# A hybrid decoder layer: the seven-product form of matrix multiplication in part of the first SwiGLU and nearly all of the second

## The chip, the cores and the metric

The kernel runs on one core of a Trainium2 chip. The metric is the device time of one execution in microseconds (us). A core has five engines that run beside each other, each in the written order of its own instructions: TensorE (PE: matrix products), VectorE (DVE), ScalarE (ACT), GpSimd (POOL) and SyncE (SP, which here issues the large transfers). They meet only by semaphores.

## The reference

The layer takes x (512 positions by 1024 features, float32) and computes, with RMSNorm as x times 1/sqrt(mean x^2 + eps) times a gain g:

```
h = x + 1/2 * SwiGLU_1(RMSNorm(x))        SwiGLU(y) = (silu(y @ w1) * (y @ w3)) @ w2
u = RMSNorm(h); y_s5, y_gla, gates from u @ W_in
h = h + W_out( sigmoid(gate_s5) * (y_s5 @ P_s5) + sigmoid(gate_gla) * (y_gla @ P_gla) )
h = h + 1/2 * SwiGLU_2(RMSNorm(h))
out = RMSNorm_final(h)
```

The hidden width is 2816, which is 22 features of 128 ("feature f" below is such a block of 128 columns of w1 and w3 with the matching 128 rows of w2). S5 is a diagonal state-space branch whose constants (discretised eigenvalues and their powers) are computed inside the kernel from its parameters; GLA is a chunked linear attention.

## The kernel before

Positions lie along the free axis, features on partitions: h is eight tiles of 128 x 512. Every product is made in split precision: an operand is written as a rounded high part and a low part (value minus high part), and `mm3` (L227) adds three matmuls: high x high, high x low, low x high. ScalarE makes the high copies and VectorE subtracts for the low ones; a subtraction that makes a weight's low part is called a low here.

The whole layer is a list of units (L63). A unit is one weight tile: it is loaded (`load`, L240, on SyncE's queue, five units ahead), split into high and low (`split`, L250, three units ahead), multiplied (`mm`), and followed by its `post`. The main loop at the end of `_body` walks the list, and this walk writes the order of each engine: at unit n it emits the load of n + 5, the matmuls of n, the split of n + 3, tasks and fetches that are due (`run_tasks`, L280), the post, and then one step of each generator that is attached to n by `side` (L978). Rings give five raw tiles, four high and four low ones, four PSUM banks `mm` and four banks `sp`.

The first SwiGLU (`ffn`, L303) takes the features in groups of 6, 6, 5 and 5 (GROUPS1). Each feature is two units, w1 and w3, of 24 matmuls of 512 columns each; behind the second stands `g_post` (L307), a chain of VectorE and ScalarE steps that applies the norm's factor b, silu and the product and splits the result into a pair. After a group its part of w2 follows: eight units, one for each tile of h. The first two of these wait for the group's last feature only with their last matmuls. The norm's factor b is asked for behind the fourth unit (`at_lead`, L424).

The S5 constants (`s5_prep`, L449) are 56 steps of small VectorE work, GpSimd copies (L608) and ScalarE copies. A step writes complex powers into one of two pairs of tiles (`cmul`, L578), and GpSimd copies out of them. The steps are spread over the units of the first SwiGLU from its seventh unit on, about one a unit.

In the second SwiGLU (`ffn_seven`, L1426) features 0 to 5 are classic and 6 to 21 use a seven-product form (Strassen and Winograd) of the 2 x 2 block product [w1; w3] by the halves of the normalized h: a feature is then seven products of 12 matmuls of 256 columns, 84 in all where the classic one has 48 of 512 columns. Its weight sums are made by VectorE tasks and its right-hand operands, called X, by `seven_x` (L1351) once, in the units behind the start of this SwiGLU; they are built from h times gain times b. The w2 parts of the group before stand between the products. The posts combine the seven results (`post_1` to `post_7`).

## Time and profile before

| | |
|---|---|
| median of 3 runs | 1068.77 us (1067.56 to 1069.32) |
| the profiled execution | 1067.78 us |
| its span in the trace | 1066.1 us |
| TensorE busy | 1052.4 us, 99% of the span |
| VectorE busy | 717.4 us, 67% |
| ScalarE busy | 438.3 us, 41% |
| GpSimd busy | 65.2 us |
| moved by DMA | 101.41 MB, 95 GB/s on average |

The span runs from the first to the last instruction that the profiler saw; 1.7 us of the execution lie outside it. Busy times of matmuls are modelled and overlap, so rates are read from starts, not from durations. The share of busy time is an average over stages: the first SwiGLU, the mixing layer, the second SwiGLU.

### The profile page before, as it was taken

What the parts mean: (1) busy time and instruction counts of PE and PEld (TensorE: products, weight loads), DVE (VectorE), ACT (ScalarE), POOL (GpSimd) and SP (SyncE); (2) the same over time, 40 slices, a digit from 0 to 9 for tenths busy, and PEclk for the clock granted to TensorE, in tenths of its full rate; (3) what the DMA queues carried; (4) which work ended last, traced back from release to release, by engine and by line L of the source; (5) the groups of instructions that cost most, each with busy time, mean ns of one, the idle gap of its engine ahead of it and who ended that gap; (6) DMA issues with size and microseconds to landing.
All of it is one profiled execution on the core that took longest, in us unless ns stands there. A gap on an engine that the chain in (4) does not pass through costs nothing.

```text
span 1066.1 us, 14475 instructions
## 1 busy us (share of the span) xinstructions
PE 1052.4 (99%) x5548; PEld 906.4 (85%) x5548; DVE 717.4 (67%) x1403; ACT 438.3 (41%) x779; POOL 65.2 (6%) x118
## 2 busy tenths in 40 slices
PE   9999999999999999999999999999999999999996
PEld 7888888888888898888878888888899999999996
DVE  6688654797644555687385755557886778777866
ACT  7323254322222433553645233434444444454444
POOL 4002600100400000001000000000000000000000
PEclk9999999999999999999999999999999999999998
DMA  7423223322422322122122222222133233333222
GB/s 260 123 61 134 79 75 103 127 85 62 149 86 62 112 102 79 60 80 79 60 80 80 80 98 99 100 79 89 60 104 105 89 110 101 107 100 109 82 78 79
DMA packets 34388, 101.41 MB, mean 95 GB/s; under 512 B 4096, under 2 KB 5568, under 8 KB 34320
## 3 DMA queue, kind: packets, MB, share of 16 engines
q1 hardware_dynamic: 33408, 99.17, 27.9%
q0 software_dynamic: 480, 0.79, 0.3%
q8 instruction: 43, 0.70, 0.3%
q10 hardware_dynamic: 432, 0.54, 0.1%
q14 instruction: 25, 0.20, 0.1%
HBM read 98.19 MB, written 2.10 MB: 94 GB/s over the span
## 4 chain that ended last, share of the span: by engine, by line
PE 95%; ACT 2%; DVE 1%; DMA 1%; issue 0%; SPq 0%; DVEq 0%; ACTq 0%
PE mm L228 20%; PE mm L230 20%; PE mm L229 20%; PE mm L1541 5%; PE mm L1540 5%; PE mm L1538 5%; PE sp L228 4%; PE sp L229 4%; PE sp L230 4%; ACT g L105 1%; PE sp L999 1%; PE sp L1001 1%; PE sp L1000 1%; PE mm L1001 1%; PE mm L1000 1%; PE mm L999 1%
## 5 line engine op out<-in xcount | busy, mean ns | idle before, releaser
L228 PE MATMUL mm<-g,hi 128*128 128x512 f32 x944 | 374.3, 396 | 0.0
L230 PE MATMUL mm<-g,lo 128*128 128x512 f32 x944 | 369.7, 392 | 0.0
L229 PE MATMUL mm<-g,hi 128*128 128x512 f32 x944 | 369.5, 391 | 0.0
L84 DVE TENSOR_TENSOR lo<-raw,hi 128x1024 fp32r<-128x1024 f32 (+3 forms) x176 | 198.6, 1133 | 130.7 <-ACT hi L105 130.3
L105 ACT ACTIVATE g<-g 128x512 f32<-128x512 f32 (+4 forms) x227 | 130.5, 582 | 338.6 <-DVE g L84 327.2
L105 ACT ACTIVATE hi<-raw 128x1024 fp32r<-128x1024 f32 (+3 forms) x176 | 170.2, 974 | 109.9 <-PE mm L229 64.5
L230 PEld LDWEIGHTS mm<-g,lo 128*128 128x128 f32 x944 | 177.7, 188 | 40.6
L229 PEld LDWEIGHTS mm<-g,hi 128*128 128x128 f32 x944 | 177.9, 188 | 37.1
L228 PEld LDWEIGHTS mm<-g,hi 128*128 128x128 f32 x944 | 177.9, 188 | 37.1
L84 DVE TENSOR_TENSOR g<-g,g 128x512 fp32r<-128x512 f32 (+7 forms) x341 | 181.6, 551 | 38.5 <-ACT g L105 32.1
L84 DVE TENSOR_TENSOR g<-mm,g 128x512 f32<-128x512 f32 (+1 forms) x104 | 58.2, 564 | 47.3 <-PE mm L1541 17.2
L228 PE MATMUL sp<-g,g 128*128 128x512 f32 (+1 forms) x176 | 65.7, 373 | 0.0
L229 PE MATMUL sp<-g,g 128*128 128x512 f32 (+1 forms) x176 | 65.4, 372 | 0.0
L230 PE MATMUL sp<-g,g 128*128 128x512 f32 (+1 forms) x176 | 65.0, 370 | 0.0
L84 DVE TENSOR_TENSOR g<-g,mm 128x512 f32<-128x512 f32 (+1 forms) x72 | 44.3, 623 | 19.7 <-PE mm L230 15.2
L105 ACT ACTIVATE g<-mm 128x256 f32<-128x256 f32 (+1 forms) x51 | 19.7, 386 | 91.4 <-PE mm L1541 78.1
L1541 PE MATMUL mm<-b,lo 128*128 128x256 f32 x192 | 53.7, 279 | 0.0
L1541 PE MATMUL mm<-g,lo 128*128 128x256 f32 x192 | 53.6, 279 | 0.0
L1538 PE MATMUL mm<-b,hi 128*128 128x256 f32 x192 | 53.6, 279 | 0.0
L1540 PE MATMUL mm<-b,hi 128*128 128x256 f32 x192 | 53.6, 279 | 0.0
L1538 PE MATMUL mm<-g,hi 128*128 128x256 f32 x192 | 53.5, 279 | 0.0
L1540 PE MATMUL mm<-g,hi 128*128 128x256 f32 x192 | 53.5, 279 | 0.0
(177 smaller groups left out, 1260.2 us busy)
## 6 DMA issues: line engine op xcount, KB each, us to landing
raw<-win SPq DMA_DIRECT2D x24, 512.0 KB, 3.4
raw<-w1b SPq DMA_DIRECT2D x22, 512.0 KB, 3.4
raw<-w3b SPq DMA_DIRECT2D x22, 512.0 KB, 3.5
raw<-w1a SPq DMA_DIRECT2D x21, 512.0 KB, 3.4
raw<-w3a SPq DMA_DIRECT2D x21, 512.0 KB, 3.6
raw<-w2b SPq DMA_DIRECT2D x32, 256.0 KB, 2.6
raw<-w2a SPq DMA_DIRECT2D x16, 384.0 KB, 3.1
raw<-w2a SPq DMA_DIRECT2D x16, 320.0 KB, 2.8
```

The lines of the kernel that those rows point to most:

```text
L84: V.tensor_tensor(out=out, in0=x, in1=y, op=op)
L105: S.activation(out, x, f, **kw)
L228: PE.matmul(out, lhsT=wh, rhs=xh, start=start, stop=False)
L229: PE.matmul(out, lhsT=wh, rhs=xl, start=False, stop=False)
L230: PE.matmul(out, lhsT=wl, rhs=xh, start=False, stop=stop)
L999: PE.matmul(banks[i], lhsT=xh, rhs=wh, start=(k == 0), stop=False)
L1000: PE.matmul(banks[i], lhsT=xh, rhs=wl, start=False, stop=False)
L1001: PE.matmul(banks[i], lhsT=xl, rhs=wh, start=False, stop=(k == KT - 1))
L1538: PE.matmul(bank, lhsT=wh[:, c], rhs=xh[k], start=start and k == 0, stop=False, skip_group_check=True)
L1540: PE.matmul(bank, lhsT=wh[:, c], rhs=xl[k], start=False, stop=False, skip_group_check=True)
L1541: PE.matmul(bank, lhsT=wl[:, c], rhs=xh[k], start=False, stop=k == 3, skip_group_check=True)
```

## The change

In the first SwiGLU features 0 to 3 stay classic, 4 to 11 take the seven-product form, and 12 to 21 are classic again in two groups of 5. The classic ones need the split x that the seven-product operands do not leave room for, so `again` reads x a second time and splits it anew. In the second SwiGLU feature 0 is classic and 1 to 21 take the seven-product form, in groups of 2, 4, 4, 4, 4 and 4. The operands X are built from h times gain, without b: in the first SwiGLU in the units from the third to the tenth, in the second beside the last product of the mixing layer. So the norm's factor has to be multiplied in behind the products: `post_2` and `post_3` get a multiplication by b before silu, and the finished value gets one too. The factor of the first norm is asked for behind the third unit rather than the fourth. The S5 preparation starts with feature 12, two steps to a unit in 28 units; its three large tiles are allocated there, since X takes their places before. Rows of w1 and w3 are stored in another order.

```diff
-GROUPS1 = [6, 6, 5, 5]
-GROUPS2 = [6, 4, 4, 4, 4]
+GROUPS1 = [4, 4, 4]
+GROUPS1_REST = [5, 5]
+GROUPS2 = [2, 4, 4, 4, 4, 4]
+ORDER_K = [0, 2, 4, 6, 1, 3, 5, 7]
+PLACE_K = [ORDER_K.index(k) for k in range(8)]
...
-    m_t, co_re, co_im = big(), big(), big()
+    m_t = co_re = co_im = None
...
-            c = k * stride + off
+            c = place[k] * stride + off
...
-    f1 = ffn(a["w1a"], a["w3a"], a["w2a"], GROUPS1, "n1", lead1, finish_ffn1)
-    at_lead(f1, "n1", 3)
...
+    def seven_x(X, g):
...
+        for j in range(4):
+            even, odd = get(), get()
+            for x, k in ((even, 2 * j), (odd, 2 * j + 1)):
+                act(x, h[k], AF.Copy, scale=g[:, k:k + 1])
+            low()
+            yield
+            ta, tb = get(), get()
+            sub(ta[:, left], even[:, right], even[:, left])
+            sub(ta[:, right], odd[:, right], ta[:, left])
+            split(even[:, left], 1, j, -1.0)
+            split(odd[:, left], 2, j)
+            yield
+            low()
+            sub(tb[:, left], even[:, right], odd[:, right])
+            sub(tb[:, right], odd[:, left], ta[:, right])
+            split(ta[:, right], 6, j)
+            split(ta[:, left], 5, j)
+            yield
+            low()
+            split(tb[:, left], 7, j)
+            split(tb[:, right], 4, j)
+            split(odd[:, right], 3, j, -1.0)
+        yield
+        low()
+        yield
+    def ffn_seven(w1, w3, w2, X, groups, classic, norm_key, lead, end):
...
+            def post_2():
+                x = v["x"] = get()
+                sub(x[:, left], v["c"][:, left], be)
+                mul(x[:, left], x[:, left], st[norm_key].b[:, left])
+                soon(1, lambda: act(x[:, left], x[:, left], AF.Silu, scale=-1.0))
...
+            def post_4():
+                x = v["x"]
+                gs[f] = pair()
+                mul(x[:, left], al, x[:, left])
+                if final:
+                    mul(x[:, left], x[:, left], st[norm_key].b[:, left])
...
+            def post_3():
+                x = v["x"]
+                add(x[:, right], ga, v["u"][:, left])
+                mul(x[:, right], x[:, right], st[norm_key].b[:, right])
+                soon(1, lambda: act(x[:, right], x[:, right], AF.Silu, scale=-1.0))
+                c = right if final else slice(0, T)
+                soon(2, lambda: (mul(x[:, right], v["c"][:, right], x[:, right]),
+                                 mul(x[:, c], x[:, c], st[norm_key].b[:, c])))
+                split_g(c, 3)
...
+        if classic == groups[0]:
+            fill = parts(0)
+            for _ in range(4):
+                next(fill)
+        for q in range(0 if fill is None else 1, len(groups)):
...
+        if end is None:
+            tail_units(w2, sum(groups[:-1]), groups[-1], gs)
+        else:
+            end()
+            for _ in parts(len(groups) - 1, 4):
+                pass
+        return first
+    def again():
+        due = len(units)
+        def fetch(k, box):
+            box.append(raws.take())
+            for i in range(2):
+                nc.sync.dma_start(out=box[0][:, i * T:(i + 1) * T], in_=a["x"][k + i])
+        def high(k, box):
+            xs[k] = pair()
+            act(xs[k][0], box[0][:, k % 2 * T:(k % 2 + 1) * T], AF.Copy, scale=g1[:, k:k + 1])
+        def low(k, box):
+            stt(xs[k][1], box[0][:, k % 2 * T:(k % 2 + 1) * T], g1[:, k:k + 1], xs[k][0].bitcast(F32), ALU.mult,
+                ALU.subtract)
+            if k % 2:
+                raws.drop(box[0])
+        for k in range(0, KT, 2):
+            box = []
+            fetches.append((due - 6 + 2 * k, [raws], lambda k=k, box=box: fetch(k, box)))
+            for i in range(2):
+                tasks.append((due + 2 + k + i, [], lambda k=k + i, box=box: high(k, box)))
+                tasks.append((due + 3 + k + i, [], lambda k=k + i, box=box: low(k, box)))
+    X1 = {}
+    f1 = ffn_seven(a["w1a"], a["w3a"], a["w2a"], X1, GROUPS1, GROUPS1[0], "n1", lead1, again)
+    at_lead(f1, "n1", 2)
+    rest1 = len(units)
+    ffn(a["w1a"], a["w3a"], a["w2a"], sum(GROUPS1), GROUPS1_REST, "n1", finish_ffn1)
...
+        nonlocal m_t, co_re, co_im
+        m_t, co_re, co_im = big(), big(), big()
...
-    f2 = ffn_seven(a["w1b"], a["w3b"], a["w2b"], GROUPS2, "n2", lead2)
+    X2 = {}
+    f2 = ffn_seven(a["w1b"], a["w3b"], a["w2b"], X2, GROUPS2, 1, "n2", lead2, None)
...
+    x1 = seven_x(X1, g1)
+    for n, times in ((2, 1), (3, 2), (4, 2), (5, 2), (6, 2), (7, 2), (8, 1), (9, 2)):
+        side(f1 + n, *[x1] * times)
+    x2 = seven_x(X2, g2)
+    for n, times in ((1, 1), (2, 1), (3, 2), (4, 1), (5, 2), (6, 1), (7, 2), (8, 2), (9, 1), (10, 1)):
+        side(mix_out + n, *[x2] * times)
...
-    spots, n = [], f1
-    for nk in GROUPS1:
-        spots.extend(range(n + 6 if n == f1 else n, n + 2 * nk - 3))
+    spots, n = [], rest1
+    for nk in GROUPS1_REST:
+        spots.extend(range(n, n + 2 * nk - 3))
         spots.extend(range(n + 2 * nk + 1, n + 2 * nk + 8))
         n += 2 * nk + 8
-    spots = spots[:-5]
...
-            o[w + s] = c(g[f"{n}_{w}"][0].reshape(8, 128, 22, 128).transpose(2, 1, 0, 3)).reshape(22, 128, 1024)
+            o[w + s] = c(g[f"{n}_{w}"][0].reshape(8, 128, 22, 128)[ORDER_K].transpose(2, 1, 0, 3)).reshape(22, 128,
+                                                                                                           1024)
```

In the program that is built the first remaining group begins at unit 112 (feature 12) and its w2 part at unit 122; the second group's units are 130 to 147.

Below is VectorE's order at two places. The names are tiles by their program number; `lo` is a low of a weight, `g` a general tile, `mm` and `sp` are PSUM banks. The first place is the S5 preparation where GpSimd copies out of the tile pair that `cmul` writes. Before (here g_862 and g_863 are one such pair, written in turn with the other half of the same tiles):

```order
L84 TENSOR_TENSOR lo_73<-raw_65,hi_69 128x1024
L84 TENSOR_TENSOR g_102<-g_102,mm_88 128x512
L84 TENSOR_TENSOR g_864<-g_862,g_472 128x256
L84 TENSOR_TENSOR g_864<-g_863,g_472 128x256
L84 TENSOR_TENSOR g_862<-g_864 128x256
L84 TENSOR_TENSOR g_864<-g_863,g_472 128x256
L84 TENSOR_TENSOR g_864<-g_862,g_472 128x256
L84 TENSOR_TENSOR g_863<-g_864 128x256
L84 TENSOR_TENSOR lo_74<-raw_66,hi_70 128x1024
L84 TENSOR_TENSOR g_103<-g_103,mm_89 128x512
L84 TENSOR_TENSOR lo_75<-raw_67,hi_71 128x1024
```

One step of six instructions stands between two lows, beside one addition to h from the w2 part. In the changed kernel, from the low of unit 121 on:

```order
L87 TENSOR_TENSOR lo_73<-raw_64,hi_69 128x1024
L87 TENSOR_TENSOR g_2440<-g_2209,g_2223 128x256 x2
L87 TENSOR_TENSOR g_2438<-g_2440 128x256
L87 TENSOR_TENSOR g_2440<-g_2209,g_2223 128x256 x2
L87 TENSOR_TENSOR g_2439<-g_2440 128x256
L87 TENSOR_TENSOR g_2440<-g_2438,g_2223 128x256
L87 TENSOR_TENSOR g_2440<-g_2439,g_2223 128x256
L87 TENSOR_TENSOR g_2438<-g_2440 128x256
L87 TENSOR_TENSOR g_2440<-g_2439,g_2223 128x256
L87 TENSOR_TENSOR g_2440<-g_2438,g_2223 128x256
L87 TENSOR_TENSOR g_2439<-g_2440 128x256
L87 TENSOR_TENSOR lo_74<-raw_65,hi_70 128x640
```

Two steps of six stand between two lows, the first two steps that write the pair from the constants c (g_2209) and onward, and behind the second low the chain of feature 15 follows.

The second place is the start of the first SwiGLU, behind the first two feature chains. Before:

```order
L84 TENSOR_TENSOR g_380<-mm_88,g_367 128x512
L96 SCALAR_TENSOR_TENSOR g_382<-mm_89,g_367 128x512
L84 TENSOR_TENSOR g_380<-g_382,g_381 128x512
L84 TENSOR_TENSOR g_388<-g_380,g_387 128x512
L84 TENSOR_TENSOR lo_72<-raw_67,hi_68 128x1024
L84 TENSOR_TENSOR g_418<-mm_90,g_367 128x512
L96 SCALAR_TENSOR_TENSOR g_420<-mm_91,g_367 128x512
```

The chain of feature 1 (four instructions on g_380), a low, and the next chain. In the changed kernel:

```order
L87 TENSOR_TENSOR g_360<-mm_85,g_347 128x512
L87 TENSOR_TENSOR g_362<-mm_86,g_347 128x512
L87 TENSOR_TENSOR g_360<-g_362,g_361 128x512
L87 TENSOR_TENSOR g_368<-g_360,g_367 128x512
L87 TENSOR_TENSOR g_371<-g_306 128x256
L87 TENSOR_TENSOR g_371<-g_307,g_371 128x256
L99 SCALAR_TENSOR_TENSOR b_375<-g_306,b_375 128x256
L87 TENSOR_TENSOR b_377<-g_307,b_377 128x256
L87 TENSOR_TENSOR g_372<-g_306,g_307 128x256
L87 TENSOR_TENSOR g_372<-g_307,g_371 128x256
L87 TENSOR_TENSOR lo_75<-raw_66,hi_71 128x1024
L87 TENSOR_TENSOR g_341<-raw_67,g_340 128x256
```

The same chain (on g_360), then six steps of 256 columns for the operands X, a low, and the first low part of a weight for product 1's feature; the next chain comes eight further instructions on.

## Rows read from the trace of the kernel before

**Rows 1.** The page's first part: busy us, share of the span, instructions of each engine.

```profile
PE 1052.4 (99%) x5548; PEld 906.4 (85%) x5548; DVE 717.4 (67%) x1403; ACT 438.3 (41%) x779; POOL 65.2 (6%) x118
```

**Rows 2.** Timeline of TensorE: start us, length, line, operation, shapes, count.

```profile
727.80 0.39 PE L229 MATMUL mm<-g,hi 128*128 128x512 f32 x1
...
744.96 0.39 PE L229 MATMUL mm<-g,hi 128*128 128x512 f32 x1
...
856.34 0.28 PE L1538 MATMUL mm<-b,hi 128*128 128x256 f32 x1
...
859.05 0.28 PE L1541 MATMUL mm<-g,lo 128*128 128x256 f32 x1
```

**Rows 3.** Windows: stretch, its length, busy us of each engine, granted clock, DMA.

```profile
850.00:900.00 50.00, 50.00 (x354) 46.76 (x353) 38.88 (x70) 24.45 (x51) 0.00 (x0) 1.00 0.28 99
```

**Rows 4.** Timelines of TensorE and VectorE at the head; idle and releaser in brackets.

```profile
18.87 0.39 PE L228 MATMUL mm<-g,hi 128*128 128x512 f32 x1
...
24.85 3.49 DVE L84 TENSOR_TENSOR lo<-raw,hi 128x1024 fp32r<-128x1024 f32 x3
...
37.54 0.69 DVE L84 TENSOR_TENSOR g<-sp,g 128x512 f32<-128x512 f32 x1 [3.20 <-ACT g L105]
...
40.94 0.68 DVE L84 TENSOR_TENSOR g<-mm,g 128x512 f32<-128x512 f32 x1
```

**Rows 5.** Timeline of VectorE: first rows of the preparation's steps 3 to 8, and ends.

```profile
60.53 0.26 DVE L84 TENSOR_TENSOR g<-s5p,g 128x16 f32<-128x16 f32 x2
...
67.15 0.58 DVE L100 TENSOR_SCALAR g<-g 128x16 f32<-128x16 f32 x3
...
69.76 0.96 DVE L84 TENSOR_TENSOR lo<-raw,hi 128x768 fp32r<-128x768 f32 x1
...
85.70 0.17 DVE L102 TENSOR_SCALAR g<-g 128x16 f32<-128x16 f32 x1
...
87.75 0.95 DVE L84 TENSOR_TENSOR lo<-raw,hi 128x768 fp32r<-128x768 f32 x1
...
89.22 0.17 DVE L100 TENSOR_SCALAR g<-g 128x16 f32<-128x16 f32 x1
...
92.07 0.95 DVE L84 TENSOR_TENSOR lo<-raw,hi 128x768 fp32r<-128x768 f32 x1
...
93.54 0.25 DVE L84 TENSOR_TENSOR g<-g 128x16 f32<-128x16 f32 x2
...
95.61 0.95 DVE L84 TENSOR_TENSOR lo<-raw,hi 128x768 fp32r<-128x768 f32 x1
...
97.07 0.75 DVE L84 TENSOR_TENSOR g<-g,g 128x256 f32<-128x256 f32 x2
```

**Rows 6.** Timelines of GpSimd and VectorE: the copies, and a write that waits for them.

```profile
98.35 27.24 POOL L608 COPY g<-g 64x64 f32<-64x64 f32 x64 [54.75 <-DVE g L84]
...
119.47 0.43 DVE L84 TENSOR_TENSOR g<-g 128x256 f32<-128x256 f32 x1 [1.51 <-POOL g L608]
```

**Rows 7.** Windows during the copies: PE, PEld, DVE, ACT, POOL busy with instructions.

```profile
98.35:103.85 5.50, 5.50 (x26) 4.52 (x25) 5.33 (x11) 1.06 (x1) 5.03 (x12) 1.00 0.43 156
...
114.85:120.35 5.50, 5.50 (x26) 4.51 (x25) 3.10 (x7) 0.83 (x2) 4.85 (x15) 1.00 0.51 186
```

**Rows 8.** Timeline of VectorE: a step of 256 columns with a squaring, and what follows.

```profile
218.38 2.47 DVE L84 TENSOR_TENSOR g<-g,g 128x256 f32<-128x256 f32 x6
...
222.24 1.22 DVE L84 TENSOR_TENSOR lo<-raw,hi 128x1024 fp32r<-128x1024 f32 x1
```

**Rows 9.** TensorE after an idle stretch, and the window behind it with its clock.

```profile
537.82 1.16 PE L904 MATMUL sp<-g,g 64*128 64x128 f32 x8 [2.45 <-ACT g L105]
...
541.40 0.63 PE L229 MATMUL mm<-g,hi 128*128 128x512 f32 x1
541.83 0.63 PE L230 MATMUL mm<-g,lo 128*128 128x512 f32 x1
...
541.00:543.00 2.00, 2.00 (x6) 1.61 (x5) 1.75 (x3) 0.22 (x1) 0.00 (x0) 0.50 0.00 0
```

More of the change, by code (lines that the diff above doesn't have):

```diff
@@ L436, in finish_ffn1, with piece, split, low @@
         finish_h(m, gm, st["nm"])
-    f1 = ffn(a["w1a"], a["w3a"], a["w2a"], GROUPS1, "n1", lead1, finish_ffn1)
-    at_lead(f1, "n1", 3)
+    def seven_x(X, g):
+        left, right = HALVES
+        lows = []
+        def piece(p, j):
+            if p in (1, 2, 6):
+                if j == 0:
+                    made[0] += 1
+                    X[p] = sb.tile([P, 4 * T], F32R, tag="big", name=f"b{made[0]}", bufs=3)
+                t = X[p]
+                return t[:, j * 256:(j + 1) * 256], t[:, 1024 + j * 256:1280 + j * 256]
+            if j % 2 == 0:
+                X[p, j // 2] = pair()
+            return tuple(t[:, HALVES[j % 2]] for t in X[p, j // 2])
+        def split(x, p, j, sign=1.0):
+            xh, xl = piece(p, j)
+            X["x", p, j] = xh, xl
+            act(xh, x, AF.Copy, scale=sign)
+            if sign == 1.0:
+                lows.append(lambda: sub(xl, x, xh.bitcast(F32)))
+            else:
+                lows.append(lambda: stt(xl, x, sign, xh.bitcast(F32), ALU.mult, ALU.subtract))
+        def low():
+            while lows:
+                lows.pop(0)()
+        for j in range(4):
[23 more added lines that the diff above has]
+        yield
@@ L1195, in mm_a @@
         def mm_a():
[L1196 to L1197 removed]
+            pa[0] = spps.get()
+            gemm(pa[0], ua, xs, range(KT - 1), KT, place=PLACE_K)
         def mm_b():
[L1200 to L1203 removed]
+            pb[0] = spps.get()
+            gemm(pb[0], ub, xs, range(KT - 1), KT, place=PLACE_K)
+            gemm(pa[0], ua, xs, [KT - 1], KT, place=PLACE_K)
+            gemm(pb[0], ub, xs, [KT - 1], KT, place=PLACE_K)
         ua.mm, ub.mm = mm_a, mm_b
@@ L1699, in _body @@
-    f2 = ffn_seven(a["w1b"], a["w3b"], a["w2b"], GROUPS2, "n2", lead2)
-    at_lead(f2, "n2", 0)
-    def x7():
-        yield from seven_x(st["n2"])
-    xgen = x7()
-    for n, times in [(2 + i, 1) for i in range(9)] + [(11, 2)]:
-        side(f2 + n, *[xgen] * times)
+    X2 = {}
+    f2 = ffn_seven(a["w1b"], a["w3b"], a["w2b"], X2, GROUPS2, 1, "n2", lead2, None)
+    at_lead(f2, "n2", 0)
+    x1 = seven_x(X1, g1)
+    for n, times in ((2, 1), (3, 2), (4, 2), (5, 2), (6, 2), (7, 2), (8, 1), (9, 2)):
+        side(f1 + n, *[x1] * times)
@@ L1752, in _body @@
     assert not tasks and not fetches and not soons
-    for gen in (prep, s5, gl, xgen):
+    for gen in (prep, s5, gl, x1, x2):
         assert next(gen, done) is done
```

508 lines of the change are left out of this document (205 added, 303 removed).

## The prediction

> **What bounds the kernel now.** I read the page's first part, then TensorE's and VectorE's timelines, then sums over windows. TensorE is busy 1052.4 of 1066.1 us, VectorE 717.4 [rows 1]. So a change pays by the TensorE time that it removes, as long as VectorE, ScalarE and GpSimd bring operands in time. That is decided stage by stage. Each engine works in its written order, so the question is how far VectorE falls behind where the change puts more before it.
>
> TensorE's rates come from starts [rows 2]: 75 steps of 512-column matmuls from 727.80 to 744.96, 0.2288 us each; 23 steps of 256-column ones from 856.34 to 859.05, 0.1178 us each. In the seven-product stage VectorE is busy 38.88 of 50 us while TensorE has no gap [rows 3].
>
> **The change, part by part.** Below, "unit n" is the n-th entry of the list of units; a classic unit is 24 matmuls, 5.49 us.
>
> *TensorE.* A classic feature is 48 x 0.2288 = 10.98 us, a seven-product one 84 x 0.1178 = 9.90. Thirteen more features go over (8 in the first SwiGLU, 5 in the second): -13 x 1.08 = -14.1 us. The Trainium skill (TensorE: Matmul & The Clock Gate, Part 1) gives start to start as columns over 2.4 GHz plus about 2.5 ns, 215.7 ns at 512; by it the saving would be an estimated 15.3 us. The measured steps are longer, and they decide.
>
> *VectorE in every seven-product feature.* Three multiplications by b are added, two of 256 columns and one of 512. Two 256-column ones take 0.75, 0.42 of that after the second starts, so 0.33 a step (from 97.07 on [rows 5]); the 512-column one is about 0.6 (the first chain's 3.40 us holds four and two waits for ScalarE [rows 4]). That is 1.27 us a feature. A feature with its share of w2 takes TensorE 9.90 + 24 x 0.2288 = 15.4 us, VectorE 0.78 of it, 12.0; now 13.3, 86%. I cost it at nothing, since TensorE covers it; if VectorE's waits for ScalarE fill the other 14%, it is the third rival.
>
> *The head.* Unit 2 starts at 18.87 [rows 4], so units 2 to 7, with the factors' matmuls (some 1.4 us), end at 53.2. VectorE's first feature chain started at 37.54 and took 3.40 [rows 4]. The factors are asked for one unit earlier, so it now starts near 32.6 (half a us of TensorE's wait for the squares' sums is in that). Until the fourth feature's chain ends, VectorE has four chains (13.6), 32 short steps for the operands X1 and the first weights (32 x 0.33 = 10.6), a low and two sums (2.3): 59.1. The w2 part that opens with features 0 to 3 reaches that feature's part at 56.6: 2.5 us of wait. Then product 1 stands at 61.3, but its operands' last low comes after seven more steps, a low and two sums (4.6): 63.7, another 2.4. Product 6 waits likewise, 1.3. With the 0.5: 6.7 us. Bounds: 0, if chains and steps overlap as the six-feature head does now, and 12, if ScalarE's copies for the steps are never in time.
>
> *The first remaining group (units 112 to 123).* The 56 steps of the S5 preparation now stand two to a unit in 28 units. I count from the end of unit 111. Feature 12's chain can start at 11.0. Behind it in VectorE's order are: chain 3.4; step 3 and a low, 60.53 to 67.15, 6.6; step 4, 2.6; step 5, 2.05; step 6, 2.85; a low of 1.13 (three take 3.49, the last 1.23 [rows 4]); the next chain 3.4; step 7, 2.07; and 1.28 until the first GpSimd copy, from 97.07 to 98.35 [rows 5, 6]. That is 36.4. From there GpSimd's 64 copies last 27.24 us without a gap [rows 6]. Before, a step's write waited for tiles that the copies read, 1.51 us until 119.47, with 6 us of copies to go [rows 6]; the next step came over a unit later and waited for nothing. Now both steps stand in unit 118, so the second one's last write waits for the last copies: 36.4 + 27.2 + 0.4 = 64.0. VectorE is held there. Behind it wait the low for unit 122 (0.7, by columns from 1.13), feature 15's chain, 68.1, another low and feature 16's, 72.2. TensorE runs units 112 to 121 meanwhile and is through at about 57; the w2 product of unit 122 needs feature 15's result, that of unit 123 feature 16's, and ends at 73.6. Without waits it would end at 10 x 5.49 + 2 x 3.43 = 61.8. Loss 11.8 us. Bounds come from the copies' speed: beside a VectorE busy 5.33 of 5.50 us GpSimd made 12 copies (0.46 us each), beside one busy 3.10 it made 15 (0.37) [rows 7]; 64 copies are then 29.3 or 23.5, and the loss 8.1 to 13.9. If VectorE's chain overlaps better before, 4 less: 4 to 14. On this the Trainium skill (Perfetto Trace Analysis, Optimizing Scalar/DVE Operations) says that GpSimd and VectorE share a read port of SBUF, so work moved between them need not run side by side. Rows 7 agree with it, and it speaks against packing copies beside a full VectorE: by it the copies would cost the estimated 2 us more.
>
> *The second remaining group (units 130 to 141).* Again two steps a unit in seven units. A step lies between 2.4 (six multiplications of 256) and 3.86 us (218.38 to 222.24) [rows 8]; I take 3.0, since most are the six or twelve alone. A unit then asks VectorE for 6.0 + 1.13 + 1.7 (half a chain) = 8.8 against 5.49: 23 us behind after seven. The lows stand three units ahead (16.5 us) and w2's first parts give 2: 4.7 us remain. Bounds 0 and 10. Units 123 to 129 and 141 to 147 have no chains in them and I cost them at nothing.
>
> *The second SwiGLU's start.* One classic feature instead of six stands between the last product of w_out and the first of the seven. The 44 operand steps move into the ten units before; they are 14.7 us beside lows, sums and squares of some 3 us a unit, 45 of 55, which fits, but the last ones and product 6's weights stand behind the norm's chain: I take 2.9, between 0 and 7.
>
> *The clock.* After 2.45 us idle at 537.82 the granted clock fell to 0.50, the lower of its two levels (1.2 of 2.4 GHz); matmuls then started 0.43 apart, and with eight of them that is 1.6 us [rows 9]. Two of the waits above are as long: 3.2; 0 to 8, if it is none or five.
>
> *Transfers.* Eight more DMAs for the second reading of x are asked for eight units ahead; nothing.
>
> *Sum:* -14.1 + 6.7 + 11.8 + 4.7 + 2.9 + 3.2 = +15.2. The profiled execution took 1067.8 (span 1066.1 and 1.7 around it): 1083.0. The median of the runs shown is 1.0 above it: **1084 us**.
>
> **The rivals.**
> *All is covered (faster).* One mechanism: VectorE's look-ahead. It works 78% of the time and four banks and lows three units ahead could hide each crowd; then only TensorE's sum counts, 1067.8 - 14.1 + 1.0 = 1054.7. It decides if the waits come to less than 14.1 together, for instance if the first group's is the lowest bound of 4 and the rest half: 1062. For it: the preparation is 56 steps that were hidden before. Against: in unit 118 VectorE waits for GpSimd, not for itself, and 27.24 us can't be hidden behind three units.
> *Even.* Waits of 12 to 16 us in all: 1068.8 by balance.
> *VectorE bounds the seven-product stage (slower still).* 86% of busy time leaves 2.1 us a feature for its waits; if these are 0.7 us too long in each of 29 features, 20 us more: 1104. For it: VectorE waits for ScalarE in every chain. Against: the stage has no TensorE gap now with 22% of VectorE free.
>
> **Chances.** Forecast 0.64, its own range 1074 to 1093. Covered 0.16; even 0.06; VectorE bound 0.14. The range that takes in half of the first and of the last: 1060 to 1098. A difference of 0.2%, about 2 us, is what a measurement of this kernel can tell from none. Faster 0.16, same 0.06, slower 0.78.
>
> **What would show it.** TensorE: 2896 products of 512 and 2632 of 256 columns where they were 3520 and 1540, at the same steps. VectorE in the remaining group: a wait for GpSimd of about 6 us or more ahead of the product's last write, then TensorE idle some 10 us at a w2 product whose releaser is VectorE, and a granted clock below 1 right behind. In the head: waits of 1 to 3 us at a w2 part and at products 1 and 6, released by VectorE. No TensorE gap in the seven-product features themselves. I am wrong if TensorE's busy share stays at 99% in the first 400 us, or if gaps stand in each seven-product feature.

## The result, and the profile after

The changed kernel takes 1100.34 us (median of 4 runs, 1099.45 to 1101.47), the kernel before 1068.24 in the same comparison (4 runs, 1067.56 to 1069.32). The ratio is 1.0298, 95% interval 1.0282 to 1.0313: slower by 32.1 us, where 15.2 were forecast. The direction and the places were right, the size was not: the median lies 2.3 us above the upper end of the range, 1098.

The page's first part, which answers to [rows 1]:

```profile
PE 1053.5 (96%) x6016; PEld 926.1 (84%) x6016; DVE 844.0 (77%) x1726; ACT 501.8 (46%) x979; POOL 63.7 (6%) x118
```

The span is 1099.0 us. TensorE is idle for 1099.0 - 1053.5 = 45.5 us of it, before for 1066.1 - 1052.4 = 13.7: the loss of 32 us is idle time. Busy time did not fall by the 14.1 us saved, because some matmuls ran at half rate (below). VectorE has 126.6 us more work.

The windows of four stretches (columns as in [rows 3]): a seven-product stretch of the second SwiGLU, then the first remaining group with GpSimd's copies, the second remaining group, and the start of the second SwiGLU:

```profile
840.00:890.00 50.00, 50.00 (x354) 46.84 (x353) 43.58 (x79) 23.98 (x51) 0.00 (x0) 1.00 0.28 85
```
```profile
250.00:290.00 40.00, 30.29 (x118) 23.92 (x117) 28.25 (x54) 11.51 (x21) 20.91 (x59) 0.87 0.24 70
...
350.00:380.00 30.00, 26.18 (x110) 20.05 (x109) 27.11 (x43) 7.99 (x12) 12.53 (x9) 1.00 0.21 57
```
```profile
740.00:760.00 20.00, 16.49 (x85) 14.88 (x84) 16.37 (x40) 12.05 (x23) 0.00 (x0) 0.77 0.09 27
```

The seven-product stretch has the same 354 matmuls in 50 us as in [rows 3] and no gap, with VectorE at 43.58/50 = 87%. The other three hold the loss. TensorE's waits (timeline of TensorE; idle and releaser in brackets), in the head:

```profile
24.10 1.05 PE L180 MATMUL sp<-cst,g 128*128 128x1 f32 x8 [1.02 <-DVE g L87]
...
60.67 0.51 PE L230 MATMUL sp<-g,g 128*128 128x512 f32 x1 [2.47 <-ACT g L108]
...
65.07 0.38 PE L600 MATMUL mm<-b,lo 128*128 128x256 f32 x1 [1.33 <-DVE lo L87]
...
70.53 0.39 PE L597 MATMUL mm<-b,hi 128*128 128x256 f32 x1 [2.05 <-ACT g L108]
...
75.47 0.38 PE L597 MATMUL mm<-g,hi 128*128 128x256 f32 x1 [1.87 <-ACT g L108]
```

in the two remaining groups (the rows at 278.17 and 278.60 follow on the wait, 0.43 apart):

```profile
256.92 0.47 PE L230 MATMUL mm<-g,hi 128*128 128x512 f32 x1 [1.85 <-DVE g L87]
...
277.61 0.77 PE L230 MATMUL mm<-g,hi 128*128 128x512 f32 x1 [7.86 <-DVE g L87]
278.17 0.63 PE L231 MATMUL mm<-g,hi 128*128 128x512 f32 x1
278.60 0.63 PE L232 MATMUL mm<-g,lo 128*128 128x512 f32 x1
...
353.24 0.50 PE L232 MATMUL mm<-g,lo 128*128 128x512 f32 x1 [1.77 <-DVE lo L87]
...
359.96 0.47 PE L230 MATMUL mm<-g,hi 128*128 128x512 f32 x1 [1.39 <-DVE g L87]
```

and in the second SwiGLU (the wait of [rows 9] at the end of the GLA branch is there as before, 2.44 us, and not shown):

```profile
735.88 0.51 PE L231 MATMUL sp<-g,hi 128*128 128x512 f32 x1 [1.76 <-DVE g L99]
...
737.88 1.05 PE L180 MATMUL sp<-cst,g 128*128 128x1 f32 x8 [1.27 <-DVE g L87]
...
753.60 0.58 PE L597 MATMUL mm<-b,hi 128*128 128x256 f32 x1 [3.51 <-ACT g L108]
753.98 0.41 PE L599 MATMUL mm<-b,hi 128*128 128x256 f32 x1
754.19 0.41 PE L600 MATMUL mm<-b,lo 128*128 128x256 f32 x1
...
819.24 0.38 PE L597 MATMUL mm<-g,hi 128*128 128x256 f32 x1 [0.88 <-DVE g L87]
```

For a sum by place I took every step from one matmul's start to the next and added up what it has above the steps of [rows 2]. A step that is long by a wait counts as idle, a run of steps near 0.43 (512 columns) or 0.213 (256) as half rate, in which TensorE runs at the lower of its two clock levels:

| place | idle | half rate | forecast (idle) |
|---|---|---|---|
| head, to 80 us | 10.5 | 3.7 | 6.7 |
| first remaining group | 10.0 | 3.6 | 11.8 |
| second remaining group | 4.3 | 0.9 | 4.7 |
| second SwiGLU's start | 7.0 | 4.6 | 2.9 |
| its second group, and the end | 2.8 | 0.2 | 0 |
| half rate, all places | | 13.0 | 3.2 |

That is 47.6, less the 14.1 saved 33.5; the span is longer by 32.9. Between fixed points, the mixing layer's norm starts at 417.13 where it was 394.41, so the first SwiGLU loses 22.7; from the matmul behind the GLA branch's wait (560.52 here, 537.82 before) to the end it is 538.4 where it was 528.3, so the second loses 10.2; the mixing layer between is the same to 0.1.

The table is of one execution. Eight more kernels below leave the head as it is, and by the same sum their heads stand idle for 7.7 to 11.1 us; so 10.5 is in the upper part of what the head does, and a difference of 2 or 3 us there between two of these kernels need not be an effect of their edits.

### The profile page after: what moved, and what is told of

Its sections match the earlier page's. It is cut to its first block, busy times and chain, and to the rows that moved or that the text cites. A ratio compares the mean times of both kernels' runs of the same rounds, so it can differ in the third digit from the quotient of the medians.

```text
span 1099.0 us, 15952 instructions
## 1 busy us (share of the span) xinstructions
PE 1053.5 (96%) x6016; PEld 926.1 (84%) x6016; DVE 844.0 (77%) x1726; ACT 501.8 (46%) x979; POOL 63.7 (6%) x118
## 4 chain that ended last, share of the span: by engine, by line
PE 70%; DVE 16%; ACT 7%; issue 3%; POOL 2%; DMA 1%; SPq 0%; DVEq 0%; POOLq 0%; ACTq 0%
DVE g L87 10%; PE mm L230 8%; PE mm L232 8%; PE mm L231 8%; PE mm L597 8%; PE mm L600 8%; PE mm L599 8%; PE sp L230 5%; PE sp L231 5%; PE sp L232 5%; ACT g L108 5%; DVE lo L87 4%; POOL g L980 2%; ACT hi L108 2%; DVE g L99 1%
## 5 line engine op out<-in xcount | busy, mean ns | idle before, releaser
L108 ACT ACTIVATE g<-g 128x512 fp32r<-128x512 f32 (+4 forms) x276 | 147.8, 546 | 356.2 <-DVE g L87 340.0
L87 DVE TENSOR_TENSOR g<-g,g 128x512 f32<-128x512 f32 (+6 forms) x474 | 244.0, 530 | 33.3 <-ACT g L108 22.2
L230 PE MATMUL mm<-g,hi 128*128 128x512 f32 x624 | 250.9, 402 | 11.2 <-DVE g L87 11.1
L87 DVE TENSOR_TENSOR lo<-raw,hi 128x1024 fp32r<-128x1024 f32 (+2 forms) x160 | 183.6, 1152 | 88.5 <-ACT hi L108 88.4
L232 PE MATMUL mm<-g,lo 128*128 128x512 f32 x624 | 247.0, 396 | 1.8 <-DVE lo L87 1.8
L231 PE MATMUL mm<-g,hi 128*128 128x512 f32 x624 | 245.5, 393 | 0.5 <-DVE g L87 0.5
L108 ACT ACTIVATE hi<-raw 128x1024 fp32r<-128x1024 f32 (+2 forms) x160 | 156.8, 986 | 37.1 <-PE mm L231 14.2
L230 PEld LDWEIGHTS mm<-g,hi 128*128 128x128 f32 x624 | 118.9, 191 | 36.8 <-issue 12.3
L231 PEld LDWEIGHTS mm<-g,hi 128*128 128x128 f32 x624 | 119.0, 191 | 26.2 <-DVE g L87 0.8
L230 PE MATMUL sp<-g,g 128*128 128x512 f32 (+1 forms) x272 | 103.2, 380 | 2.5 <-ACT g L108 2.5
L597 PE MATMUL mm<-b,hi 128*128 128x256 f32 x348 | 98.9, 284 | 5.6 <-ACT g L108 5.6
L231 PE MATMUL sp<-g,g 128*128 128x512 f32 (+1 forms) x272 | 103.0, 379 | 0.2 <-DVE g L87 0.2
L232 PE MATMUL sp<-g,g 128*128 128x512 f32 (+1 forms) x272 | 102.4, 376 | 0.0
L597 PE MATMUL mm<-g,hi 128*128 128x256 f32 x348 | 98.9, 284 | 3.2 <-ACT g L108 2.3
L599 PE MATMUL mm<-b,hi 128*128 128x256 f32 x348 | 98.8, 284 | 0.3 <-DVE b L99 0.3
L599 PE MATMUL mm<-g,hi 128*128 128x256 f32 x348 | 98.1, 282 | 0.0
L108 ACT ACTIVATE g<-mm 128x256 f32<-128x256 f32 (+1 forms) x90 | 34.4, 383 | 117.7 <-PE mm L600 104.5
```

The lines of the kernel that those rows point to most:

```text
L87: V.tensor_tensor(out=out, in0=x, in1=y, op=op)
L108: S.activation(out, x, f, **kw)
L230: PE.matmul(out, lhsT=wh, rhs=xh, start=start, stop=False)
L231: PE.matmul(out, lhsT=wh, rhs=xl, start=False, stop=False)
L232: PE.matmul(out, lhsT=wl, rhs=xh, start=False, stop=stop)
L597: PE.matmul(bank, lhsT=wh[:, c], rhs=xh, start=start and k == 0, stop=False, skip_group_check=True)
```

## The experiments

Each kernel is the changed one with the edit shown (long edits are cut at "..."); each ratio is to the kernel before, run in the same batch on the same chip, with its 95% interval. These intervals are about 2 us wide on either side, so two of these kernels that differ by 2 us are not told apart by their times.

### Which SwiGLU, and which of its parts

**first_before**: the first SwiGLU is the old one, the second the changed one.

```
-    f1 = ffn_seven(a["w1a"], ..., GROUPS1, GROUPS1[0], "n1", lead1, again)
+    f1 = ffn(a["w1a"], ..., 0, [6, 6, 5, 5], "n1", finish_ffn1, lead1)
```

> The changed kernel with the whole first SwiGLU classic, in groups of 6, 6, 5 and 5, the factor asked for behind the fourth unit and the S5 preparation spread over it about one step a unit, as before the change; the second SwiGLU stays the changed one. Theory (the first SwiGLU loses 14.3 us at its head, 13.6 and 5.2 at its two remaining groups, idle and half clock together, and saves 8.6): 1100.3 - 33.1 + 8.6 = 1076 (1073 to 1079). Rival (the loss is spread over the seven-product features): it would give back at most 10 us beyond the 8.6, 1090 or more.

1079.13 us, ratio 1.0092 (1.0071 to 1.0114), at the upper end of what the theory gave, 0.1 us above it; the rival is out. The three waits at the second SwiGLU's start are the same in its trace (1.76, 1.27 and 3.51 us).

**second_before**: the second SwiGLU has six classic features again, and the operand steps stand beside them; the first is the changed one.

```
-GROUPS2 = [2, 4, 4, 4, 4, 4]
+GROUPS2 = [6, 4, 4, 4, 4]
```

> The changed kernel with six classic features at the start of the second SwiGLU, groups of 6, 4, 4, 4 and 4 and the operand steps beside the classic features, but the operands still without b and the multiplications by b behind the products. Theory (the start of the second SwiGLU costs 7.0 us idle, 4.6 at half clock and 1.9 at the second group): these 13.5 go, five features of 1.08 us come back, 1100.3 - 13.5 + 5.4 = 1092 (1090 to 1095). Rival (the multiplications by b slow every seven-product feature, the start is only where it shows): five features less at half a us each, 1100 + 5.4 - 2.5, 1101 to 1104.

1090.53 us, ratio 1.0203 (1.0185 to 1.0220). The two gave back 21.2 and 9.8; 1100.3 less both is 1069.3, the kernel before. So the losses add up and do not act on each other. In second_before the new operands, without b, are used in sixteen features, and the time from behind the GLA branch's wait to the end is 529.5, 1.3 above before: the form itself costs little. The rest comes with the five further features, whose operand steps have to stand ahead of the norm.

**no_b**: no multiplication by b in the seven-product features; the output lacks the factor there.

```
-                mul(x[:, left], x[:, left], st[norm_key].b[:, left])
...
-                mul(x[:, right], x[:, right], st[norm_key].b[:, right])
```

> The changed kernel without the multiplications by the norm's factor in the seven-product features; its output leaves that factor out there. Theory (TensorE covers them, and they stand behind the waits at the starts): 1098 to 1101, with the same idle stretches. Rival (they set the pace of the 29 seven-product features at about half a us each): 14 us less, 1084 to 1088.

1095.79 us, ratio 1.0252 (1.0231 to 1.0273), between the two expectations: 4.5 us. In its trace the wait at 819 is gone, and from the sum for the second SwiGLU's norm to the end it takes 359.1 us where the changed kernel takes 361.1, 1.9 less. So the multiplications cost where VectorE is behind already; the steady seven-product stretch of the first SwiGLU, from 80 to 253 us, takes the same to 0.1 us without them. The other 2.6 us have no place of their own: the head is 4.5 us shorter, but it is 4.0 us shorter in c_tiles too, which has the multiplications.

### The second SwiGLU's start

TensorE waits 3.51 us at 753.60 for ScalarE. ScalarE's timeline ahead of it:

```profile
747.51 0.58 ACT L108 ACTIVATE g<-sp 128x512 f32<-128x512 f32 x1
748.10 1.28 ACT L108 ACT_TABLE_LOAD   x1
749.40 0.63 ACT L108 ACTIVATE g<-g 128x512 f32<-128x512 f32 x1
...
750.78 1.55 ACT L108 ACTIVATE g<-g 128x512 fp32r<-128x512 f32 x4 [0.76 <-DVE g L87]
...
753.18 0.36 ACT L108 ACTIVATE g<-mm 128x256 f32<-128x256 f32 x1
```

The last row copies product 1's bank, which product 6 needs. It is a third of a us of work, but it stands in ScalarE's order behind feature 0's chain: the norm's factor, a table load, silu, and high copies that wait for VectorE. In the head product 6 waits 2.05 us at 70.53 for the same kind of copy:

```profile
70.12 0.36 ACT L108 ACTIVATE g<-mm 128x256 f32<-128x256 f32 x1
```

**late_chain**: feature 0's chain is written behind product 6's post.

```
+    chain0 = units[f2 + 1].post
+    units[f2 + 1].post = None
...
+    post6 = units[f2 + 4].post
+    units[f2 + 4].post = lambda: (post6(), chain0())
```

> The changed kernel, but in the second SwiGLU the chain of feature 0 (norm's factor, silu, product, split) is written behind product 6 of feature 1 instead of ahead of product 1. Theory (product 6 waits 3.51 us because ScalarE's copy of product 1's bank stands behind that chain in ScalarE's order): this wait goes or falls under 0.7, and with it the half-clock stretch behind it (2.7 us): 1100.3 - 5.5 = 1095 (1093.5 to 1097). Rival (product 6 waits for VectorE, which is behind by its operand steps): the wait stays over 2.5 us, 1099 to 1101.

1096.99 us, ratio 1.0264 (1.0243 to 1.0285). The wait fell to 0.28 us, with a new one of 1.76 for the same kind of copy, now of product 7's bank, ahead of the same feature's product 4:

```profile
750.54 0.38 PE L597 MATMUL mm<-b,hi 128*128 128x256 f32 x1 [0.28 <-ACT g L108]
...
758.13 0.39 PE L597 MATMUL mm<-g,hi 128*128 128x256 f32 x1 [1.76 <-ACT g L108]
```

So the place in ScalarE's order is shown as the cause of this wait. By the medians 3.4 of the second SwiGLU's 10 us came back, and by the traces 4.0 (from the norm's sum to the end 357.1 us for 361.1), at the upper edge of the range expected.

### The first remaining group

**c_tiles**: the four steps that write behind GpSimd's copies get tiles of their own.

```
+        own = [get(), get()]
...
-            o_re, o_im = v3(e_re[i % 2]), v3(e_im[i % 2])
+            o_re, o_im = (v3(x[:, i % 2 * 256:i % 2 * 256 + 256]) for x in own)
```

> The changed kernel, but the four S5 steps that multiply the constants c write into two tiles of their own instead of the pair that GpSimd still copies out of. Theory (VectorE is held in unit 118 by GpSimd's last copies): the two idle stretches of 1.85 and 7.86 us at the first remaining group's w2 part shrink by 7 to 8 us, the half-clock stretch behind them by 1 to 3 us, the time comes to 1090 to 1093. Rival (VectorE simply has too much work there, whoever it waits for): it reaches the two feature chains as late as before, less than 3 us gained, 1097 to 1100.

1096.96 us, ratio 1.0253 (1.0230 to 1.0277). VectorE's four waits for GpSimd, in the changed kernel

```profile
265.24 0.43 DVE L87 TENSOR_TENSOR g<-g 128x256 f32<-128x256 f32 x1 [0.68 <-POOL g L980]
...
268.01 0.42 DVE L87 TENSOR_TENSOR g<-g 128x256 f32<-128x256 f32 x1 [1.51 <-POOL g L980]
...
270.84 0.42 DVE L87 TENSOR_TENSOR g<-g 128x256 f32<-128x256 f32 x1 [1.58 <-POOL g L980]
...
273.64 0.42 DVE L87 TENSOR_TENSOR g<-g 128x256 f32<-128x256 f32 x1 [1.54 <-POOL g L980]
```

(5.3 us in all), are gone, and TensorE's wait behind them fell from 7.86 to 3.29:

```profile
269.04 0.48 PE L230 MATMUL mm<-g,hi 128*128 128x512 f32 x1 [3.29 <-DVE g L87]
```

By the medians 3.4 us came back, and 4.7 between fixed points (under spread36); both lie between the two expectations. The copies are a part of this wait. Another part is not VectorE's work either: in both kernels VectorE then stands idle for 1.97 us, right ahead of feature 15's chain, for ScalarE's high copy of unit 122's weight. Changed kernel, and then c_tiles:

```profile
274.09 1.14 ACT L108 ACTIVATE b<-g 64x256 f32<-64x256 f32 x3 [2.38 <-DVE g L87]
275.26 0.74 ACT L108 ACTIVATE hi<-raw 128x640 fp32r<-128x640 f32 x1
...
276.03 0.83 DVE L87 TENSOR_TENSOR lo<-raw,hi 128x640 fp32r<-128x640 f32 x1 [1.97 <-ACT hi L108]
```
```profile
267.44 0.84 DVE L87 TENSOR_TENSOR lo<-raw,hi 128x640 fp32r<-128x640 f32 x1 [1.97 <-ACT hi L108]
```

The high copy stands in ScalarE's order behind the preparation's own copies (L108, 64x256), which wait for the step's last write. No run moved it, so this part is read from the traces and not tested.

### The clock: cause or consequence

**warm**: matmuls that nobody reads, ahead of the fourth part of unit 122 (32 of them) and ahead of the second SwiGLU's first product 6 (14).

```
+            for _ in range(n):
+                PE.matmul(bank[:, 0:P], lhsT=idle, rhs=idle, start=True, stop=True)
```

> The changed kernel with extra matmuls whose result nobody reads, written where TensorE waits longest: 32 of 128 columns ahead of the fourth part of unit 122 (wait 7.86 us) and 14 ahead of product 6 of the second SwiGLU's first seven-product feature (3.51 us). Theory (the granted clock falls because TensorE stood idle, and the fall costs about 3.6 and 2.7 us there): no stretch at half clock behind the two places, time 1100.3 - 6 = 1094 (1092 to 1097). Rival (the clock falls for another reason, or the extra matmuls only push the work back): 1099 or more.

1107.32 us, ratio 1.0346: missed. The wait is at the unit's first matmul, for the bank that feature 15's chain reads, not in its fourth part as I had it. So the filler ran behind the wait and added its own 7.4 us (each of the 32 calls is two instructions in the trace).

**warm_before**: the filler stands ahead of unit 122's first matmul.

> The changed kernel with the unread matmuls once more, 14 ahead of product 6 as in the run before, and the 32 now ahead of the first matmul of unit 122, where the wait of 7.86 us lies (for the bank that feature 15's chain frees), instead of behind it. Theory (the granted clock falls because TensorE stands idle): both places run on at 2.4 GHz, the steps behind them at 0.229 and 0.118 us; 3.6 + 2.7 us less, 1092 to 1096. Rival (the clock falls for another reason): steps of 0.43 us behind unit 122's wait, 1097 or more.

1099.36 us, ratio 1.0293 (1.0275 to 1.0311). Its windows behind the two waits, and then those of the changed kernel:

```profile
278.00:284.00 6.00, 5.55 (x23) 4.21 (x24) 4.85 (x8) 2.73 (x5) 0.00 (x0) 1.00 0.39 108
...
754.00:760.00 6.00, 5.01 (x43) 4.81 (x43) 5.90 (x12) 2.72 (x6) 0.00 (x0) 1.00 0.29 90
```
```profile
278.00:284.00 6.00, 6.00 (x20) 4.71 (x20) 4.40 (x8) 2.99 (x6) 0.00 (x0) 0.70 0.35 104
...
754.00:760.00 6.00, 6.00 (x32) 6.00 (x32) 5.90 (x11) 2.36 (x5) 0.00 (x0) 0.55 0.30 90
```

The granted clock stayed at 1.00 where it was 0.70 and 0.55, so at these two places it fell because TensorE stood idle, as the theory said. But TensorE is no longer busy throughout: in part it waits instead. The medians differ by 1.0 us (1.8 with each kernel against its own comparison), which is not told from none, and not by the 4 to 8 expected. The traces say more, if the same two matmuls are taken in both kernels. From 268.67 to 298.71 the changed kernel takes 30.04 us, with filler 29.34: 0.7 back. From 747.57 to 765.75 it takes 18.18, with filler 16.82: 1.4 back. The half rate right behind these two waits was 1.9 and 2.7 us above the full rate (nine steps from 277.61, 27 from 753.60). (The 3.6 us of the expectation take in the stretch behind the wait at 256.92, where no filler stood.) So somewhat under half came back. The remainder of the slow matmuls stood where a wait for operands would have stood: VectorE is busy 5.90 of 6 us at the second place, with filler and without, and with it new waits stand there, the longest 0.99 us at 757.76. At these two places half rate is thus only in part a cost of its own; the others were not tried.

### Order or amount of VectorE's work

**prep_early**: seven of the preparation's 56 steps stand in the seven-product stage, with the tiles of c_tiles; the large tiles are allocated at the eighth step.

```
+    for n in (20, 44, 68, 90, 99, 103, 107):
+        side(n, prep)
```

> The changed kernel with the seven first steps of the S5 preparation (small VectorE steps that need no large tile) in units 20 to 107 of the seven-product stage, the other 49 over the same 28 units, the large tiles taken at the eighth step, and own tiles for the four steps of the constants c. Theory (what the two remaining groups lose is VectorE's crowd there, GpSimd's copies being a part of it): the first group's 9.7 us idle and 3.6 at half clock fall under 2 together, the second group's 5.2 stays about, no new wait over 1 us in the seven-product stage: 1100.3 - 12 = 1088 (1085 to 1091). Rival (the first group's wait is GpSimd's 27 us of copies alone): no better than own tiles alone, 1096 to 1098.

1097.10 us, ratio 1.0256 (1.0238 to 1.0274), no gain over c_tiles: the time is the rival's, but the trace is the theory's for the first group. From 215 to 285 us TensorE is busy 69.57 of 70, so the first group's waits are gone, but new ones came in the seven-product stage, such as

```profile
131.80 0.39 PE L597 MATMUL mm<-g,hi 128*128 128x256 f32 x1 [1.32 <-DVE g L87]
```

and the second group's grew (2.41 and 2.57 us at 340 and 348).

**spread36**: the 56 steps of c_tiles over all 36 units of the two groups. **spread36_early**: that, and the seven early steps too.

```
-        spots.extend(range(n, n + 2 * nk - 3))
-        spots.extend(range(n + 2 * nk + 1, n + 2 * nk + 8))
+        spots.extend(range(n, n + 2 * nk + 8))
```

> The changed kernel with own tiles for the constants c (as in the run before) and the 56 steps of the S5 preparation over all 36 units of the two remaining groups instead of 28. From the last seven-product matmul of the first SwiGLU to the mixing layer's norm the changed kernel takes 231.0 us, with own tiles 226.3. If the order decides (two steps a unit beside the chains): under 221, time 1088 to 1092. If the amount of VectorE's work decides: 224 or more, 1095 to 1098.

> As the run above, and the seven first steps of the preparation in units 20 to 107 of the seven-product stage. If the amount in the two groups decides, seven steps less make them shorter than in the run above by 4 us or more, and the seven-product stage keeps the 3 to 5 us of waits that these steps cost there: 1092 to 1096. If the order decides, the groups stand at their floor already (under 219) and the seven-product stage's waits come on top: 1090 to 1094, not better than the run above.

1094.96 us (1.0238, 1.0216 to 1.0256) and 1090.36 us (1.0191, 1.0168 to 1.0213). From the last matmul of the last product 4 of the first SwiGLU (2.9 us ahead of its last seven-product matmul) to the mixing layer's norm it is 231.0 us in the changed kernel, 226.3 in c_tiles, 227.3 in spread36, 223.3 in prep_early and 214.9 with both edits. A thinner spread alone does nothing here, though neither of the two theories says why. The wait at unit 122 is gone in spread36, but TensorE waits for GpSimd at a transposition that belongs to the preparation itself:

```profile
270.13 1.12 PE L1000 MATMUL sp<-idn,g 128*128 128x128 f32 x4 [4.62 <-POOL g L980]
```

It reads what GpSimd copies, and the copies last from 245.24 to 272.58 there. With the seven early steps the copies start at 224.74 and that wait is gone. Less work in the old spread takes 3.0 off c_tiles; with both edits it is 11.4, and one wait of 0.5 us is left. So neither the order nor the amount decides by itself, and the time of 1090.36 us is below what the amount's theory gave. But the seven steps cost the stage that took them in 5 to 8 us of new waits (from the first seven-product matmul to the same product 4 it is 119.7 us in c_tiles, 125.3 in prep_early, 127.7 with both). From 90 to 185 us VectorE is busy 81.49 of 95 us in the changed kernel, 86%; seven steps were already too many there.

**six_first**: six classic features ahead instead of four, so that only eight remain for the preparation.

```
-GROUPS1 = [4, 4, 4]
-GROUPS1_REST = [5, 5]
+GROUPS1 = [6, 4, 4]
+GROUPS1_REST = [4, 4]
```

> The changed kernel with six classic features ahead in the first SwiGLU instead of four (groups 6, 4 and 4, then 4 and 4 classic), the operand steps over ten units instead of eight and the factor asked for behind the fourth unit; as many seven-product features as the changed kernel. Theory (the head waits because VectorE has to make the operands within eight units): the head's 10.5 us idle fall under 3 and its 3.7 at half clock under 1; the preparation is crowded into 24 units instead of 28 and its two groups lose more, 3 to 8 us: 1100.3 - 11 + 5 = 1094 (1090 to 1098). Rival (the head waits for the norm's factor and ScalarE's copies whatever the room): its idle stays over 8 us, 1102 or more.

1103.00 us, ratio 1.0313 (1.0295 to 1.0331): missed. The head's idle time fell from 10.5 to 2.6 us as expected, but the preparation in 24 units lost at least as much, in waits of 5.47, 7.10 and 6.54 us (the second at a transposition of the preparation, for ScalarE).

### A version between the two

The first SwiGLU as before, four, three or two classic features ahead of the second (classic4, classic3, classic2); with two also with feature 0's chain written late, as in late_chain (classic2_late). The operand steps move along: they begin two, four and seven units ahead of the second SwiGLU. The edit of classic2, in part:

```
-GROUPS2 = [2, 4, 4, 4, 4, 4]
+GROUPS2 = [6, 4, 4, 4, 4]
...
-    f2 = ffn_seven(a["w1b"], a["w3b"], a["w2b"], X2, GROUPS2, 1, "n2", lead2, None)
+    f2 = ffn_seven(a["w1b"], a["w3b"], a["w2b"], X2, GROUPS2, 2, "n2", lead2, None)
```

> The first SwiGLU classic as before the change, in the second SwiGLU four classic and 18 seven-product features (groups 6, 4, 4, 4 and 4), operands without b, their steps over ten units. Theory (each feature that changes its form saves 1.08 us as long as VectorE's operand steps have room; the form without b costs 0.8 us in all): from the run with six classic features, 532.9 us from the mixing layer's late matmuls to the end, two features less: 530.7, time 1067 to 1068, a gain over the kernel before of 0.5 to 2 us. Rival (any start with fewer classic features waits): 1070 or more.

> The same with three classic features and the operand steps from four units ahead of the second SwiGLU on. Theory: 1.08 us less than with four if VectorE's steps still fit, 1066 to 1068. Rival (the wait for the norm's chain in ScalarE's order, 3.5 us with one classic feature, comes back): 1070 to 1073.

> The same with two classic features and the operand steps beside the mixing layer's last product, as in the changed kernel but a unit longer. Theory (the idle 1.76 and 1.27 us come from operand steps ahead of the last split of h and of the norm's sum, whatever the number of classic features; the 3.51 us from the chain of feature 0 ahead of ScalarE's copy, which is long done with one more feature): 1.08 us less than with three, 3 us idle and up to 2 at half clock more: 1068 to 1071. Rival (the extra feature clears all waits): 1065 to 1066.

> The first SwiGLU as before the change, two classic features in the second, and the chain of feature 0 written behind product 6 of feature 2. Theory (ScalarE's order makes product 6 wait, 1.08 us idle of it left with two classic features): that wait under 0.4, time 1 us below the run without the move: 1069 to 1070.5. Rival (feature 1's chain stands there as well and VectorE is behind anyway): no change, 1070 to 1071.5.

1072.68 (1.0031, 1.0020 to 1.0042), 1073.41 (1.0037, 1.0023 to 1.0051), 1070.68 (1.0012, 1.0002 to 1.0022) and 1072.82 us (1.0031, 1.0019 to 1.0044). None beats the kernel before: each feature moved saves 1.08 us and the waits that the earlier operands bring take that and a little more. The expected 1067 to 1068 was too hopeful for four and three; with three the longest wait, 2.58 us, is for VectorE and not for ScalarE as the rival had it. With two the time came out as expected, but by luck: the waits of 1.76 and 1.27 us for the norm, which were to stay, shrank to one of 0.35,

```profile
712.49 1.05 PE L180 MATMUL sp<-cst,g 128*128 128x1 f32 x8 [0.35 <-DVE g L87]
```

and others of 1.08 and 1.24 us, ahead of products 6 and 7 for copies by ScalarE, took their place. Ahead of the second SwiGLU classic2 has nine operand steps where the changed kernel has ten, so one step less there may be what clears these two waits; no run moved that step alone. The late chain missed both expectations: the old wait fell from 1.08 to 0.64, a new one of 2.00 us for a copy by ScalarE came ahead of product 4, and the time is 2.1 us longer, not shorter:

```profile
743.89 0.54 PE L599 MATMUL mm<-g,hi 128*128 128x256 f32 x1 [2.00 <-ACT g L108]
```

## Why the prediction was right in direction and wrong in size

*Right.* TensorE's term, -14.1: the steps and the count of matmuls are as forecast, and the seven-product stretches have no gap at 87% (86 forecast), so the rival by which VectorE bounds that stage falls. The first remaining group: 10.0 us idle where 11.8 stood. GpSimd's copies begin 36.4 us behind the end of unit 111, to the tenth as forecast. But the wait for GpSimd is 5.3 us in four pieces, not 6 ahead of one write; TensorE's loss is divided between two waits, and the longer falls on the first matmul of unit 122, not on its fourth part. c_tiles shows that GpSimd held 4.6 us of that wait (7.86 to 3.29); 1.97 of what is left is VectorE's wait for ScalarE's high copy, which the forecast did not have. The 64 copies took 26.46 us (27.2 forecast):

```profile
247.14 26.46 POOL L980 COPY g<-g 64x64 f32<-64x64 f32 x64 [40.62 <-DVE g L87]
```
The second remaining group: 4.3 for 4.7. Here the sum fits better than the picture: a backlog that grows over seven units was forecast, and there are separate waits of 1.77, 1.39 and 0.53 us.

Two steps failed: the wait at the second SwiGLU's start, which was looked for on the wrong engine, and the clock's term, which is the largest error of the sum.

*The second SwiGLU's start, the step that failed in its mechanism.* "I take 2.9, between 0 and 7": the measured idle time is 7.0, and 4.6 at half rate with it. I counted VectorE's load by units (45 of 55 us) and found that it fits. The longest wait, 3.51 of the 7.0, was not for VectorE's load but for one short ScalarE copy, which stands behind a chain of 5.7 us from 747.51 on (late_chain). I had put the norm's chain down as something that delays product 6's weights, and did not follow ScalarE's order to the copy that clears the bank.

*The clock, the step that failed most in size.* "3.2; 0 to 8": 13.0 are measured in the same reckoning. I counted two waits as long as that of [rows 9] and eight matmuls behind each. Six stretches of half rate came, of 1.6 to 2.7 us each, and waits as short as 1.02 us (at 24.10) and 1.85 (at 256.92) stood ahead of them; behind product 6 it is 27 steps. warm_before shows that filling two of these places returns 2.1 of 4.6 us, so the rest covers time that VectorE and ScalarE needed. As a term it was too small by 9.8 us; as a cause about half of it counts, where it was tried.

*The head.* 6.7 forecast, 10.5 idle. The chains came about as forecast: the first at 33.46 (32.6), the fourth over at 61.3 (59.1):

```profile
33.46 1.29 DVE L87 TENSOR_TENSOR g<-sp,g 128x512 f32<-128x512 f32 x2 [3.96 <-ACT g L108]
...
60.65 0.69 DVE L87 TENSOR_TENSOR g<-g,g 128x512 fp32r<-128x512 f32 x1 [0.76 <-ACT g L108]
```

The w2 part, product 1 and product 6 wait in the forecast order, 2.47, 1.33 and 2.05; but the first and the last of them are released by ScalarE, where the forecast had VectorE for all. What is missing are the wait of product 7 (1.87, for ScalarE too) and a longer one for the squares (1.02 for 0.5). By the eight other executions with this head the error is 1.0 to 4.4 us.

*The multiplications by b, costed at nothing.* 4.5 us (no_b). They are covered in the steady stretches, as I said, but from the second SwiGLU's norm on they cost 1.9 us; where the rest comes from is not shown.

In sum: the second start +8.7 with its half rate, the head +3.8, half rate elsewhere +5.2, the waits from 819 on +2.8, and the two groups -2.2 make 18.3, which is the 33.5 of the table less the 15.2 forecast; the medians differ by 16.9. The term of 5.2 is the softest: how half rate and waits would divide without each other was tried at two places only. The head's 3.8 is of one execution.

## What to carry to other kernels

Work that moves from TensorE to VectorE is free only in the stages where VectorE has room; count the work that was hidden in the units that the change takes away, because it has to go into fewer ones. For each short copy that clears an accumulation bank, look at what stands ahead of it in its engine's order: here one of a third of a us behind a chain of 5.7 us cost TensorE 3.5. The same holds for the high copy that a low waits for. Moving a crowd can move the wait with it: seven steps and a thinner spread took 11.4 us out of two groups here and put 8 into the stage that received the steps. And half rate can follow a wait of 1 us as well as the longest ones; how much of it is a cost of its own, only a run shows.

## What was not expected of the hardware

Idle stretches of like length left different rates. In the changed kernel matmuls of 512 columns start 0.43 apart behind the 7.86 us that end at 277.61, but 0.24 apart one us behind the 2.47 us that end at 60.67; behind 1.02 us that end at 24.10, and eight matmuls of one column, they are 0.42 apart:

```profile
25.97 0.63 PE L230 MATMUL mm<-g,hi 128*128 128x512 f32 x1
26.39 0.63 PE L231 MATMUL mm<-g,hi 128*128 128x512 f32 x1
...
61.73 0.40 PE L232 MATMUL sp<-g,g 128*128 128x512 f32 x1
61.97 0.39 PE L230 MATMUL sp<-g,g 128*128 128x512 f32 x1
```

[Rows 9] has 0.43 behind an idle stretch of 2.45 us, so the length alone does not tell. The Trainium skill (TensorE: Matmul & The Clock Gate, Part 1) gives, for the lower level, a start-to-start time of columns over 1.2 GHz, 426.7 ns at 512; the two rows at 278.17 and 278.60 agree with 0.43.

In warm_before, matmuls that nobody reads filled 7.30 us of unit 122's wait, and the granted clock behind it was 1.00; the next matmuls start 0.31 and 0.24 apart:

```profile
270.35 7.30 PE L323 MATMUL sp<-idle 128*128 128x128 f32 x64
...
278.36 0.47 PE L230 MATMUL mm<-g,hi 128*128 128x512 f32 x1 [0.71 <-DVE g L87]
278.67 0.40 PE L231 MATMUL mm<-g,hi 128*128 128x512 f32 x1
278.91 0.39 PE L232 MATMUL mm<-g,lo 128*128 128x512 f32 x1
```

That the upper level then returned less than half of what the lower one had taken, because the operands were late, was the larger surprise.
